# A list schedule that reckons transfers on one shared wire, and eight idle matmuls instead of twelve

## The chip, the cores and the metric

The kernel runs on one core of one Trainium2 chip. The metric is the device time in microseconds; several runs are taken, and their median counts. The core has five instruction streams, each carried out strictly in the order in which the program holds it: TensorE (PE in the profile, with PEld for its weight loads), VectorE (DVE), ScalarE (ACT), GpSimd (POOL) and SyncE (SP). SP and ACT issue the transfers (DMA) from HBM. The streams wait for one another by semaphores.

## What is computed

Two layers of a small transformer on 256 positions of width 1024, in float32. Each layer has a normalisation whose scale, shift and gate come from a conditioning vector `c` (`ada_w`, 1024 × 3072 per layer), a mixer, and a gated residual. The first mixer (nsa) has 16 heads in 4 groups and adds up three attentions: over compressed blocks, over selected blocks and over a window. With 256 positions the selection takes every block. The second (moba) is plain causal attention at this length.

```python
cond = jax.nn.silu(c)
for i in range(DEPTH):                       # DEPTH = 2
    shift, scale, gate = jnp.split(cond @ ada_w[i] + ada_b[i], 3, axis=-1)
    h = rms_norm(x, norm_g[i]) * (1 + scale[:, None, :]) + shift[:, None, :]
    y = nsa_mixer(h, ...) if i % 2 == 0 else moba_mixer(h, ...)
    x = x + gate[:, None, :] * y
# nsa_mixer: q, kc, vc, ks, vs, kw, vw, gl, z = split(h @ w_in)
#   o = g0 * attend(q, compressed) + g1 * attend(q, selected) + g2 * attend(q, window)
# moba_mixer: q, k, v, z = split(h @ w_in);  o = attend(q, k, v)
# both: y = (o * silu(z)) @ w_out
```

## The kernel before

**The work.** Every weight matrix is read from HBM once, in pieces of 256 rows by 512 columns (512 KB) that land in a tile of the ring `raw` (five buffers; `early`, twelve, in the first stage). ACT casts a piece into its high part `hi` (float32r), DVE subtracts to get the low part `lo` (function `parts_of`), and PE multiplies three times: high by high, low part of the weight, low part of the activation `HT`. Rings of four buffers hold `hi` and `lo`. Products add up in PSUM, in the ring `acc` (two buffers: one pair, for the two halves of the positions) or `ps` (six). Function `chunk` takes one slice of 512 output columns through four pieces and then lets ACT copy both accumulators out (for the queries by `raw_part`, into `n_in`); the next chunk needs the two buffers again. The second layer's gate is computed beside the chunks on DVE, from eight more pieces of `ada_w` (`ada_gate`). So the stream of `raw` loads in the second layer alternates between `moba_w_in` and `ada_w`.

**The stages**, as the trace shows them: conditioning, first normalisation and first products (to about 60 us); keys, compression and the rest of the first layer's projections, mixed with the attention of the first layer (to about 190); output projection and second normalisation (to about 230); the second layer's projections (to about 270), attention (to about 310) and output projection.

**What sets the order.** Nothing is issued while the program is described. Class `Plan` records every operation with its engine, a cost in nanoseconds (`_cost`), what it depends on and the tiles that it needs. At the end `Plan.issue` runs a list schedule: each engine has a clock; again and again the operation that can start first by the model is taken (equal starts are decided by a level and then by the order of description), its engine's clock is moved on, and the real instruction is emitted. The engine then holds its instructions in that order for good. The model's times decide nothing but the order and which buffer of a ring a tile gets; at run time an instruction waits for its real semaphores. All instructions are emitted at one line, L354, so the profile names nearly everything L354, and tiles tell operations apart.

In the model an operation's result is seen by others some time after its end (`SEEN`, by engine: T, A, V, G, S are PE, ACT, DVE, POOL, SP). A transfer takes up its issuing engine's clock for its bytes at 360 bytes per nanosecond, at least 450 ns, and its data is seen `SEEN["S"]` later. What waits on SP for another operation gets a hop of 1,220 ns. `START` is each clock's beginning. A ring's buffer is free again when its last reader is done, by the model.

```python
SEEN = {"T": 197.0, "A": 142.0, "V": 128.0, "G": 200.0, "S": 910.0}            # L60
START = {"T": 1500.0, "A": 2000.0, "V": 1500.0, "G": 5800.0, "S": 1750.0}       # L62
return max(450.0, free(aps[0]) * aps[0].shape[0] * 4 / 360.0)                   # _cost of a transfer
seen = end + (self.SEEN["S"] if "dma" in op["calls"][0][0] else self.SEEN[e])   # L332, issue
```

**The idle matmuls.** Twelve multiplications of the 128 × 128 identity by itself into a PSUM tile that nobody reads (`SPINS`, L425) fill PE before there is work. They are recorded at the lowest urgency, so the schedule puts them where PE would else wait. The trace shows each as two matmul records, 24 in all: ten from 1.41 us, six from 4.05 us and eight from 8.46 us.

Of the kernel before, what the change touches and what calls it, by code (L numbers as in the profile page):

```python
# [18 lines left out]
S = 256  # L19
# [15 lines left out]

TICK = 10240 / 3
TILED, LATER = -0.5, 0


class Tag:  # L40
# [9 lines left out]
class Plan:  # L50
# [6 lines left out]

    SEEN = {"T": 197.0, "A": 142.0, "V": 128.0, "G": 200.0, "S": 910.0}  # L60
    AHEAD = 250.0
    START = {"T": 1500.0, "A": 2000.0, "V": 1500.0, "G": 5800.0, "S": 1750.0}  # L62

    def __init__(self, nc):
        self.nc = nc
# [86 lines left out]
    def record(self, engine, method, args, kw):  # L152
        op = self.open or self._new(engine)
        op["engine"] = op["engine"] or engine
        assert op["engine"] == engine
        aps = [a for a in list(args) + list(kw.values()) if isinstance(a, bass.AP)]
        outs = [aps[0]] + ([kw["accum_out"]] if "accum_out" in kw else [])
        for a in aps:
            if not any(a is o for o in outs):
                self._touch(op, a, False)  # L160
        for a in outs:
            self._touch(op, a, True)
        op["calls"].append((method, args, kw))
        op["cost"] += self._cost(engine, method, args, kw, aps)
        if engine == "T":
            op["mode"] = (aps[1].shape[0], aps[1].shape[-1]) if "tile_position" in kw else None
        return op

    def _cost(self, engine, method, args, kw, aps):
        def free(a):  # L170
            n = 1
            for _, k in a.ap[1:]:
                n *= k
            return n

        if "dma" in method:
            return max(450.0, free(aps[0]) * aps[0].shape[0] * 4 / 360.0)
        psum = any(str(a.space).endswith("PSUM") for a in aps)
        n = max(free(a) for a in aps)
        if engine == "T":  # L180
            if method == "transpose":
                return 262.0 if aps[1].dtype == F32 else 180.0
            cols = free(aps[2])
            if aps[2].dtype == F32:
                m = free(aps[1])
                if "tile_position" in kw and m <= 64:
                    return max(cols * 4.28 * max(32, m) / P, 60.0)
                return 2 * max(cols * 2.14, 264.0)
            return max(cols * (1.07 if aps[2].dtype == F32R else 1.0), 264.0)
        if engine == "A":  # L190
            return 0.833 * n + (51.0 if psum else 94.0) + 93.0 * sum(isinstance(kw.get(k), bass.AP) for k in ("bias", "scale", "accum_out"))
        if engine == "G":
            return 1.5 * n + 150.0
        if method == "reciprocal":
            return 6.5 * n + 68.0
        fast = not psum and (method == "tensor_copy" or method.startswith("tensor_scalar"))
        pointers = len(aps) - 2 if method.startswith("tensor_scalar") else 0
        return (0.521 if fast else 1.042) * n + 68.0 + 61.0 * pointers
# [22 lines left out]
    def issue(self, opening=()):  # L221
# [40 lines left out]
                return None  # L262
            return max(min(tag.free)[0], gate["end"] if gate else 0.0)

        clock = dict(self.START)
        tally, mode = {}, None
        ready = {e: [] for e in self.engines}
        for op in ops:
# [4 lines left out]
        while done < len(ops):  # L273
            best = None
            for e, ops_e in ready.items():
                if not ops_e:
                    continue
                found = []
                first = None
                for op in ops_e:  # L280
                    t = max(clock[e], op["at"])
                    if first is not None and t > first and not (op["level"] < 0 and t <= first + self.AHEAD):
                        continue
                    blocked = False
                    for n in op["needs"]:
                        r = room(n)
                        if r is None:
                            blocked = True
                            break
                        t = max(t, r)  # L290
                    if blocked:
                        continue
                    found.append((t, self._rank(op, e, mode), op["id"], op))
                    first = t if first is None else min(first, t)
                pick = min(found, key=lambda f: f[:3]) if found else None
                if pick:
                    soon = [f for f in found if f[1] < 0 and f[1] < pick[1] and f[0] <= pick[0] + self.AHEAD
                            and f[0] < pick[0] + pick[3]["cost"]]
                    if soon:
                        pick = min(soon, key=lambda f: (f[1], f[0], f[2]))  # L300
                if pick and (best is None or pick[0] < best[0]):
                    best = pick + (e,)
            start, _, _, op, e = best
            ready[e].remove(op)
            for n in op["needs"]:
                t = self.tiles[n]
                if t["slot"] is None:
                    tag = t["tag"]
                    gate = closed.get(tag.name)
                    if gate and not gate["called"]:  # L310
                        gate["called"] = True
                        gate["call"]()
                    slot = min(tag.free)
                    tag.free.remove(slot)
                    t["slot"] = slot[1]
                    tag.given.add(t["place"])
                    tag.early.add(t["place"])
                    while tag.next in tag.given:
                        tag.early.discard(tag.next)
                        tag.next += 1  # L320
                    tag.known.clear()
            cost = op["cost"]
            if e == "T":
                tick = int(start // TICK)
                if op["mode"] != mode:
                    cost += 240.0
                mode = op["mode"]
                cost = cost * (1 / 2.4 if tally.get(tick - 1, 0.0) >= 3060.0 else 1 / 1.2)
                tally[tick] = tally.get(tick, 0.0) + op["cost"]
            end = start + cost  # L330
            clock[e] = end
            seen = end + (self.SEEN["S"] if "dma" in op["calls"][0][0] else self.SEEN[e])  # L332
            op["end"], op["begin"] = seen, start
            for n in op["needs"]:
                t = self.tiles[n]
                t["left"] -= 1
                t["end"] = max(t["end"], seen)
                if not t["left"]:
                    t["tag"].free.append((t["end"], t["slot"]))
                    t["tag"].early.discard(t["place"])  # L340
                    t["tag"].done.add(t["place"])
                    t["tag"].known.clear()
                    for g in gates:
                        if t["tag"].name in g["for"]:
                            g["left"] -= 1
                            g["end"] = max(g["end"], t["end"])
            for a in after[op["id"]]:
                b = ops[a]
                b["at"] = max(b["at"], end if e == b["engine"] == "T" else seen + (1220.0 if b["engine"] == "S" else 0.0))
                b["wait"] -= 1  # L350
                if not b["wait"]:
                    ready[b["engine"]].append(b)
            for method, args, kw in op["calls"]:
                r = getattr(self.engines[e], method)(*[self._real(a) for a in args],  # L354
                                                     **{k: self._real(a) for k, a in kw.items()})
            done += 1
# [25 lines left out]
def kernel(  # L382
# [29 lines left out]
    T, A, V, G, Q = plan.T, plan.A, plan.V, plan.G, plan.S  # L412
# [9 lines left out]
        late["pool"] = ctx.enter_context(tc.tile_pool(name="attn", bufs=1))  # L422

    KP = 2
    SPINS = 12  # L425
    START = [("s", 0, 1), ("k", 0), ("s", 1, 1), ("s", 2, 2), ("k", 1), ("s", 4, 2), ("k", 2), ("s", 6, 2), ("k", 3)]
    plan.tag("acc", psum, 512, 2, space="PSUM")
    plan.tag("ps", psum, 512, 6, space="PSUM")
# [474 lines left out]
    FIRST = ((1024, 512), (1536, 512), (2048, 512), (0, 256))  # L903
    load_stage(*START[0])
    load_stage(*START[1], range(2))
    load_stage(*START[2])
    load_stage(*START[1], range(2, 4))
    for _ in small_loads():
# [166 lines left out]
    for kq in range(4):  # L1075
        w1 = [load(bass.AP(tensor=nsa_cmp_w1.tensor, offset=nsa_cmp_w1.offset + kv * 2048 * 256 + kq * 512 * 256,
                           ap=[[256, P], [P * 256, 4], [1, 256]])) for kv in range(2)]
        for k in range(4):
            with plan.at(FILL), plan.group():
                for kv in range(2):  # L1080
                    T.matmul(hid[64 * kv:64 * kv + 64, 0:256],
                             FLAT[kv][kq // 2][:, 4 * (kq % 2) + k].rearrange("p g n -> p (g n)"), w1[kv][:, k, :],
                             start=(kq == 0 and k == 0), stop=(kq == 3 and k == 3), tile_position=(0, 64 * kv))
# [20 lines left out]
    with plan.group():  # L1104
        for cc in range(2):
            T.matmul(cmp_ps[0:64, 0:64], u[:, cc, 0, :], w2[:, 0, cc, :], start=(cc == 0), stop=(cc == 1))
        for m in range(2):
            T.matmul(cmp_ps[0:64, 64:96], selC[:, m].rearrange("p g n -> p (g n)"), TCS[:, m, :],
                     start=(m == 0), stop=(m == 1))
# [22 lines left out]
    for hf in range(2):  # L1132
        for cc in range(2):
# [4 lines left out]
                     start=(cc == 0), stop=(cc == 1))  # L1138
# [237 lines left out]
```

## Time and profile before

| | |
|---|---|
| median of 3 runs | 340.52 us (338.61 to 341.25) |
| the profiled execution's own time | 338.96 us |
| its span, first to last instruction | 337.2 us |
| mean granted TensorE clock | 0.995 |
| busy time of PE, DVE, ACT, POOL | 319.1, 238.8, 195.8, 27.6 us |
| matmul records | 2143 |
| moved by DMA | 66.84 MB, 198 GB/s over the span |

The profile is of one execution. Times are microseconds from the first instruction of the span. In a row of the timeline stand start, duration, engine, line, operation, output and inputs by tile name, shapes and count; in square brackets the engine's idle time just before it and what ended it. In the table of waits stand the engine and tile that waited, what for, and the total, number and longest of the waits. The chain that ended last gives start, duration and what took the time. Matmuls overlap, so a matmul's duration is longer than its distance to the next one: products of 512 columns follow one another every 0.23 us.

### The profile page before, as it was taken

The page shows a single profiled execution, that of the slowest core. Times are in us where ns is not written, and L with a number is a line of the kernel's source. Part 1 is how long each engine was busy: PE and PEld are TensorE (multiplying, and loading weights), DVE is VectorE, ACT ScalarE, POOL GpSimd, SP SyncE. Part 2 cuts the span into 40 slices and gives each one's busy share as a digit, 9 for nine tenths or more (in the row PEclk, how much of TensorE's full clock was granted, in tenths as well). Part 3 has the DMA queues.
Part 4 walks back from the last instruction along what each step waited for, and adds up shares of the span by engine and source line. Part 5 has one row for each costly group of instructions (what it writes and reads, how often), then busy time and mean ns, then how long its engine had stood idle before and what let it go on. Part 6 is the DMA issues. An engine that isn't in the chain of part 4 may idle for free.

```text
span 337.2 us, 5948 instructions
## 1 busy us (share of the span) xinstructions
PE 319.1 (95%) x2143; PEld 252.5 (75%) x2143; DVE 238.8 (71%) x569; ACT 195.8 (58%) x467; POOL 27.6 (8%) x97
## 2 busy tenths in 40 slices
PE   5899999999999889999999999989869999999994
PEld 4675677796577557977979887767657998889883
DVE  1544465789889671986855587897978999974763
ACT  4625235546586555655885673886255799884420
POOL 6000898000000000000000000000000000000000
PEclk9999999999999999999999999999979999999999
DMA  8979998646985492476826338248896330303102
GB/s 252 339 252 367 366 363 276 195 135 211 353 281 213 150 385 77 140 235 225 290 75 240 82 115 278 87 133 280 296 345 200 124 124 1 126 0 137 51 34 93
DMA packets 43876, 66.84 MB, mean 198 GB/s; under 512 B 3799, under 2 KB 20294, under 8 KB 43846
## 3 DMA queue, kind: packets, MB, share of 16 engines
q1 hardware_dynamic: 43678, 66.40, 59.0%
q8 instruction: 17, 0.28, 0.3%
q14 instruction: 13, 0.11, 0.1%
q10 hardware_dynamic: 168, 0.06, 0.1%
HBM read 65.40 MB, written 1.05 MB: 197 GB/s over the span
## 4 chain that ended last, share of the span: by engine, by line
PE 76%; DMA 9%; DVE 8%; ACT 4%; issue 1%; ACTq 1%; SPq 0%; DVEq 0%
PE ps L354 43%; PE acc L354 33%; DMA raw<-in_nsa_w_in_dram 4%; DVE lo L354 2%; DMA y<-in_nsa_cmp_pe_dram 2%; DMA raw<-in_moba_w_in_dram 1%; DMA raw<-in_ada_w_dram 1%; ACT hi L354 1%; ACT p L354 1%; DVE gate L354 1%; DVE tiny L354 1%; DVE rs L354 1%; ACT n_in L354 1%; DVE y L354 1%; ACTq L354 1%
## 5 line engine op out<-in xcount | busy, mean ns | idle before, releaser
L354 ACT CAST hi<-raw 128x1024 fp32r<-128x1024 f32 (+1 forms) x50 | 50.9, 1026 | 35.2 <-PE acc L354 19.2
L354 DVE TENSOR_TENSOR lo<-raw,hi 128x1024 fp32r<-128x1024 f32 (+1 forms) x50 | 59.0, 1185 | 15.7 <-ACT hi L354 15.6
L354 PE MATMUL acc<-hi,HT 128*128 128x512 f32 (+1 forms) x176 | 58.1, 396 | 5.6 <-ACT n_in L354 3.7
L354 PE MATMUL acc<-HT,hi 128*128 128x256 f32 x256 | 51.2, 291 | 0.0
L354 ACT ACTIVATE p<-ps,tiny 128x128 f32<-128x128 f32 (+1 forms) x96 | 39.6, 431 | 11.6 <-DVE tiny L354 11.5
L354 PEld LDWEIGHTS acc<-hi,HT 128*128 128x128 f32 x176 | 33.0, 192 | 15.2 <-ACT n_in L354 4.1
L354 PEld LDWEIGHTS acc<-HT,hi 128*128 128x128 f32 x256 | 40.5, 189 | 1.3 <-DVE g L354 0.8
L354 PE MATMUL acc<-HT,lo 128*128 128x256 f32 x128 | 36.7, 288 | 0.0
L354 PE MATMUL acc<-lo,HT 128*128 128x512 f32 (+1 forms) x88 | 35.5, 404 | 0.3 <-DVE lo L354 0.3
L354 DVE TENSOR_REDUCE tiny<-ps 128x2 f32<-128x512 f32 (+2 forms) x40 | 24.8, 628 | 11.1 <-PE ps L354 10.8
L354 PE MATMUL ps<-KTA,qg 128*128 128x256 f32 (+1 forms) x192 | 30.7, 297 | 0.0
L354 PE MATMUL ps<-hi,HT 128*128 128x512 f32 (+1 forms) x96 | 28.6, 367 | 0.0
L354 PEld LDWEIGHTS ps<-KTA,qg 128*128 128x128 f32 x192 | 26.2, 191 | 2.7 <-issue 1.8
L354 ACT COPY pT<-ps 128x384 f32<-128x384 f32 x48 | 21.1, 497 | 9.2 <-PE ps L354 9.1
L354 PEld LDWEIGHTS acc<-HT,lo 128*128 128x128 f32 x128 | 24.2, 189 | 0.3 <-issue 0.2
L354 PE MATMUL ps<-hi,qg 128*128 128x512 f32 x64 | 22.2, 395 | 0.0
L354 PE MATMUL acc<-hi,qg 128*128 128x512 f32 x64 | 22.0, 394 | 0.0
L354 PE MATMUL ps<-identF,p 128*128 128x128 f32 x144 | 20.7, 276 | 0.3 <-ACT p L354 0.3
L354 ACT ACTIVATION_READ_ACCUMULATOR p<-ps,tiny 128x1 f32 x96 | 20.7, 215 | 0.0
L354 PEld LDWEIGHTS ps<-hi,HT 128*128 128x128 f32 x96 | 17.1, 188 | 4.3 <-issue 1.9
L354 PEld LDWEIGHTS acc<-lo,HT 128*128 128x128 f32 x88 | 17.0, 193 | 3.9 <-DVE lo L354 1.2
L354 PE MATMUL ps<-pT,VA 128*64 128x256 f32 (+1 forms) x192 | 18.9, 334 | 0.0
(194 smaller groups left out, 563.3 us busy)
## 6 DMA issues: line engine op xcount, KB each, us to landing
raw<-in_ada_w_dram SPq DMA_DIRECT2D x32, 512.0 KB, 5.1
raw<-in_moba_w_in_dram SPq DMA_DIRECT2D x20, 512.0 KB, 4.7
early<-in_ada_w_dram SPq DMA_DIRECT2D x16, 512.0 KB, 10.0
early<-in_nsa_w_in_dram SPq DMA_DIRECT2D x12, 512.0 KB, 8.9
raw<-in_nsa_w_in_dram SPq DMA_DIRECT2D x12, 512.0 KB, 5.6
raw<-in_nsa_cmp_w_dram SPq DMA_DIRECT2D x8, 512.0 KB, 4.2
raw<-in_nsa_w_out_dram SPq DMA_DIRECT2D x8, 512.0 KB, 4.9
raw<-in_moba_w_out_dram SPq DMA_DIRECT2D x8, 512.0 KB, 4.2
```

Source lines behind the costliest of these rows:

```text
L354: r = getattr(self.engines[e], method)(*[self._real(a) for a in args], **{k: self._real(a) for k, a in kw.items()})
```

## The change

The model of transfers in `Plan` is replaced. An issue takes 450 ns on ACT whatever its size, and on SP the bytes at 330 bytes per nanosecond, at least 450 ns. A clock `wire`, shared by all transfers, says when the data has passed: not before 450 + 1,500 ns after the start of the issue, and one transfer behind the other at 330 bytes per nanosecond; the data is seen 700 ns after that. The extra hop of 1,220 ns into SP is gone. Results of ACT and DVE are seen 20 ns later than before; ACT and SP begin at 790 ns. `SEEN["S"]` is no longer what a transfer's landing is taken from. And `SPINS` is 8 instead of 12. Apart from the four idle matmuls no operation is added or removed: the same ones are put in an order that the new model gives.

```diff
+ISSUE, FIRST_BYTE, RATE, LANDED = 450.0, 1500.0, 330.0, 700.0
...
-    SEEN = {"T": 197.0, "A": 142.0, "V": 128.0, "G": 200.0, "S": 910.0}
+    SEEN = {"T": 197.0, "A": 162.0, "V": 148.0, "G": 200.0, "S": 200.0}
     AHEAD = 250.0
-    START = {"T": 1500.0, "A": 2000.0, "V": 1500.0, "G": 5800.0, "S": 1750.0}
+    START = {"T": 1500.0, "A": 790.0, "V": 1500.0, "G": 5800.0, "S": 790.0}
...
+        if "dma" in method:
+            op["bytes"] = self.bytes
...
         if "dma" in method:
-            return max(450.0, free(aps[0]) * aps[0].shape[0] * 4 / 360.0)
+            self.bytes = free(aps[0]) * aps[0].shape[0] * 4
+            return ISSUE if engine == "A" else max(ISSUE, self.bytes / RATE)
...
-        clock = dict(self.START)
+        clock, wire = dict(self.START), 0.0
...
-            seen = end + (self.SEEN["S"] if "dma" in op["calls"][0][0] else self.SEEN[e])
+            seen = end + self.SEEN[e]
+            if "bytes" in op:
+                wire = max(wire, start + ISSUE + FIRST_BYTE) + op["bytes"] / RATE
+                seen = wire + LANDED
...
-                b["at"] = max(b["at"], end if e == b["engine"] == "T" else seen + (1220.0 if b["engine"] == "S" else 0.0))
+                b["at"] = max(b["at"], end if e == b["engine"] == "T" else seen)
...
-    SPINS = 12
+    SPINS = 8
```

## The prediction

> **What bounds the kernel now.** First the page's head, for which engine is full.
>
> ```profile
> span 337.2 us, 5948 instructions
> ...
> PE 319.1 (95%) x2143; PEld 252.5 (75%) x2143; DVE 238.8 (71%) x569; ACT 195.8 (58%) x467; POOL 27.6 (8%) x97
> ```
>
> TensorE (PE) is busy for 319.1 of 337.2 us. A new order of the same matmuls can win only what is left, 18.1 us, and what PE loses while busy. Where that lies is read from the table of windows: microseconds, then busy time of each engine, the granted PE clock, the DMA share and GB/s.
>
> ```profile
> core 0: us, PE busy (x) PEld busy (x) DVE busy (x) ACT busy (x) POOL busy (x), PEclk, DMA share, GB/s
> 0.00:20.00 20.00, 14.60 (x119) 12.08 (x120) 8.12 (x31) 11.10 (x19) 5.17 (x32) 1.00 0.89 273
> 20.00:80.00 60.00, 59.97 (x387) 44.72 (x388) 37.00 (x81) 25.35 (x43) 22.47 (x65) 1.00 0.85 275
> 80.00:130.00 50.00, 46.85 (x326) 32.37 (x324) 38.64 (x110) 31.28 (x89) 0.00 (x0) 1.00 0.76 263
> 130.00:210.00 80.00, 80.00 (x607) 66.11 (x604) 54.73 (x127) 50.85 (x139) 0.00 (x0) 1.00 0.54 179
> 210.00:240.00 30.00, 28.70 (x127) 21.42 (x127) 25.70 (x52) 20.91 (x46) 0.00 (x0) 1.00 0.56 181
> 240.00:247.20 7.20, 3.52 (x16) 2.54 (x14) 5.95 (x11) 2.73 (x4) 0.00 (x0) 1.00 0.97 354
> 247.20:252.00 4.80, 4.80 (x15) 3.75 (x16) 4.47 (x9) 2.96 (x4) 0.00 (x0) 0.65 0.90 334
> 252.00:331.00 79.00, 79.00 (x553) 68.50 (x552) 62.47 (x152) 50.56 (x127) 0.00 (x0) 1.00 0.28 92
> 331.00:337.30 6.30, 1.67 (x8) 1.03 (x6) 1.76 (x3) 0.00 (x0) 0.00 (x0) 1.00 0.22 83
> ```
>
> PE is idle for 5.4 us at the start, 3.2 us from 80 to 130, 1.3 us from 210 to 240, 3.7 us from 240 to 247, and 4.6 us at the end, where the last output is written. From 247.2 to 252 it has 0.65 of its clock, which costs 0.35 × 4.8 = 1.7 us more. Everywhere else it never stops. PE's waits from 80 to 130, and from 236 to 262 (total, times, longest):
>
> ```profile
> PE ps L354 <- ACT p L354: 1.2, 2, 0.9
> PE acc L354 <- DMA raw<-in_nsa_cmp_w_dram: 0.6, 1, 0.6
> PE ps L354 <- DVE pc L354: 0.6, 1, 0.6
> PE acc L354 <- ACT hi L354: 0.5, 1, 0.5
> PE acc L354 <- DVE lo L354: 0.3, 1, 0.3
> ```
>
> ```profile
> PE acc L354 <- ACT n_in L354: 3.7, 1, 3.7
> ```
>
> The last one is the largest. PE at both ends of it, ACT in the meantime, and from the chain and the table of transfers the two loads ahead:
>
> ```profile
> 243.03 0.39 PE L354 MATMUL acc<-hi,HT 128*128 128x512 f32 x1
> 247.10 0.50 PE L354 MATMUL acc<-hi,HT 128*128 128x512 f32 x1 [3.68 <-ACT n_in L354]
> ```
>
> ```profile
> 241.87 1.05 ACT L354 CAST hi<-raw 128x1024 fp32r<-128x1024 f32 x1 [3.30 <-DMA raw<-in_moba_w_in_dram]
> 245.52 1.04 ACT L354 CAST hi<-raw 128x1024 fp32r<-128x1024 f32 x1 [2.60 <-DVE gate L354]
> 246.47 1.07 ACT L354 COPY n_in<-acc 128x512 f32<-128x512 f32 x2
> ```
>
> ```profile
> 237.24 4.53 DMA raw<-in_moba_w_in_dram
> ```
>
> ```profile
> raw<-in_moba_w_in_dram SPq DMA_DIRECT2D x1, 512.0 KB, 5.2
> ```
>
> PE finished the `acc` pair at 243.42 and needed a free one. ACT had been free since 242.92, but the next instruction in its fixed order was a cast of a weight tile. That tile's load was issued at 240.24 (the last row is that one load, 5.2 us to landing), so it landed at 245.4. The cast is put down to a gate instruction that ended then too. Both evictions of `acc` stood behind it. This is an error of the planner's order, and its size can be read: before, the schedule takes such a load for 524,288 / 360 + 910 = 2,366 ns. The rows show 4.5 and 5.2 us. The same between 108 and 122 us:
>
> ```profile
> 108.54 4.93 DMA raw<-in_nsa_w_in_dram
> ...
> 115.88 3.73 DMA raw<-in_nsa_w_in_dram
> ```
>
> ```profile
> 113.55 1.05 ACT L354 CAST hi<-raw 128x1024 fp32r<-128x1024 f32 x1 [2.01 <-DMA raw<-in_nsa_w_in_dram]
> ...
> 119.64 1.05 ACT L354 CAST hi<-raw 128x1024 fp32r<-128x1024 f32 x1 [1.32 <-DMA raw<-in_nsa_w_in_dram]
> ```
>
> ACT stands 2.0 and 1.3 us in front of casts whose loads took 4.9 and 3.7 us, with softmax exponentials queued behind them; PE's waits for `p` and `pc` (1.2 + 0.6 us) follow.
>
> **The change part by part.**
>
> *Later landings.* A 512 KB load is now reckoned 450 + 1,500 + 524,288 / 330 + 700 = 4,239 ns from issue to landing, 1,873 ns more. Against the four rows above (3.7 to 5.2 us) the old figure is 1.4 to 2.8 us early, the new one 0.5 us late to 1.0 us early. No instruction is added or removed. Loads of `raw` are all issued from SP in program order within one ring of five buffers, so SP's order can hardly change; what changes is where casts (ACT), low parts (DVE) and products (PE) stand among other work.
>
> (1) The wait at 243. If the second cast comes behind the evictions, these run once PE is done: the first `acc` (its last matmul is six before the end, 6 × 0.23 = 1.4 us earlier) after the cast that ends at 242.92, free near 243.5. The pause falls from 3.7 to about 0.3 us, and the 1.7 us of slow clock behind it goes. What is late next: PE then has two pieces at hand, cast at 237.5 and 241.87, of 12 matmuls each, 2 × 12 × 0.23 = 5.5 us, to 249.1; the third is cast at 245.52 and is ready. From 252 to 331 PE never stops, so an earlier start should carry to the end. Bounds: 0 (the order stays) to −5.4. I take −5.0, nearest the row, since old landings undershoot by 2.8 us here.
>
> (2) Waits from 80 to 130: 1.8 us behind the casts, 0.8 us for `hi` and `lo`, 0.6 us for a load itself. Bounds 0 to −3.2. A new belief of 4.2 us does not cover a load of 4.9, and the 0.6 us is a transfer that stays late: I take −1.5, near half.
>
> (3) *Hops 20 ns longer* (ACT, DVE), the hop of 1,220 ns into SP dropped, ACT and SP begun at 790 ns. The two queues' first transfers do start at 0.79 in the trace. The dropped hop touches the four output writes, which nothing follows on SP. These only break ties: 0, with (5).
>
> (4) *Eight idle matmuls for twelve.* Each is two records.
>
> ```profile
> 8.46 1.96 PE L354 MATMUL ps<-identF 128*128 128x128 f32 x8
> 10.36 1.94 PE L354 MATMUL ps<-early,condz 128*32 128x128 f32 x32
> 12.22 1.50 PE L354 MATMUL ps<-identF,n_in 128*128 128x128 f32 x8
> 13.56 0.28 PE L354 MATMUL ps<-selP,row 128*128 128x2 f32 x2
> 13.70 1.07 PE L354 MATMUL ps<-identF,n_in 128*128 128x128 f32 x8
> ```
>
> ```profile
> 11.04 0.75 DVE L354 TENSOR_SCALAR n_in<-X,rs 128x1024 f32<-128x1024 f32 x1
> ```
>
> The last four, 1.96 us, run just ahead of the modulation matmuls. Without them those could start near 8.7, but the transposes of `n_in` wait for DVE until 11.79, so at most 12.22 − 11.79 = 0.4 us reaches the path. Against it: eight transposes take 1.50 us and the next eight 1.07 us, so PE gets faster near 13, and less work before may put that off. The nearest price is the 1.7 us that the slow stretch at 247 cost. Bounds −0.4 to +1.7; I take 0, as PE mostly waits for others there.
>
> The Trainium skill, "TensorE: Matmul & The Clock Gate", Part 1 (the warmup section), speaks against this part: the clock stays halved until about 3.4 us of sustained activity, in a free-running window. The speed-up near 13 us and the 0.65 clock after 3.7 us of idling agree with it; by that rule a missed window would make the sum 1.7 us longer.
>
> (5) *New waits.* Every engine's order is rebuilt, and a new order has mistakes of its own. Of today's PE idle between 20 and 331 us (0.03 + 3.15 + 1.30 + 3.68 = 8.2 us), 3.7 + 1.8 + 0.8 = 6.3 us come from early casts, and 1.9 us from other causes. Bounds 0 to +5.4 (one more wait like that at 243); I take +1.5, near those 1.9.
>
> Sum: −5.0 − 1.5 + 0 + 0 + 1.5 = −5.0 us. The profiled execution took 338.96 us (its span and 1.76 us around it), so 334.0; the runs' median, 340.52, is 1.56 us above it, so the forecast for the median is 335.5. The three runs lie within 338.6 to 341.25, so under 1% (3.4 us) can hardly be told from no change.
>
> **The rivals.**
>
> - *Casts and evictions move together* (the change does not do what it says). Around 240 us the transfers run at a 0.97 share, so every landing may move in the plan and PE's end of the chunk with it; the cast stays in front. For it: both depend on the same stream of loads. Against: PE had two cast pieces in hand, so its end does not hang on the newest load. Waits stay; part (2) alone and new waits cancel: 340.0.
> - *A colder start*: part (4) at its worst, +1.7: 335.5 + 1.7 = 337.2. For: the speeds at 12 and 13.7 us. Against: nothing on PE is urgent until 16 us.
> - *Casts too late, loads starved*: slower. A raw buffer is given back after cast and low part; if these now stand behind chain work, the next load is issued later.
>
> ```profile
> raw<-in_moba_w_in_dram SPq DMA_DIRECT2D x13, 512.0 KB, 4.9
> raw<-in_ada_w_dram SPq DMA_DIRECT2D x7, 512.0 KB, 4.4
> ```
>
> Between 221 and 260 us 20 loads go out through five buffers, four rounds. If each round slips by the 1.87 us of added belief, 7.5 us come on top, in place of the 3.7 us wait: 340.5 + 7.5 − 3.7 = 344.3. It decides from where the slip per round passes the wait that it replaces, 3.7 / 4 = 0.9 us. For: the share of 0.97 leaves no slack. Against: loads really take 4.4 to 5.2 us, longer than the new belief, so casts are still placed rather early than late.
> - *All order waits go and nothing new comes*: 3.7 + 1.7 + 1.8 + 0.8 = 8.0 us less, 332.5.
>
> **How the numbers follow.** Chances: forecast 0.46 (its own range 332 to 338.5), together 0.25, starved 0.14, colder start 0.10, all gone 0.05. The likeliest is the forecast, 335.5. A range of 331 to 343 leaves out the starved case's larger half and a little below 331. Faster by over 1% (below 337.1): 0.44 of the forecast's 0.46, all of "all gone", half of the colder start, hardly any of "together": 0.55. Within 1%: the rest of these two and most of "together": 0.30. Slower (above 343.9): most of "starved" and the worst of "together": 0.15.
>
> **What would show it.** Right: near 243 us an eviction of `acc` on ACT ahead of the cast that waits longest, no PE wait of over 1 us from 236 to 260, granted clock 1.00 there, ACT's waits for loads from 104 to 126 shorter than 3.3 us in all, PE busy still near 317 to 318 (four idle matmuls less). Wrong: a wait of the old size at a new place, PE idle between loads from 225 to 260 with a DMA share under 0.8, or the second eight transposes still at 1.5 us.

## The result, and the profile after

The changed kernel takes 330.75 us (median of 4, 329.93 to 331.21), the kernel before 340.29 (median of 4 beside it): ratio 0.972, 95% interval 0.968 to 0.977. The forecast was 335.5, with a range of 331 to 343: the result lies 0.25 us below the range; the direction and the wait at 243 us came as forecast, the size did not. Times and ratios from here on leave out one execution each of the kernel before (342.95 us), spins_only (342.12) and landed_m1173 (349.07), which fell into a slower state of the chip. Between the two profiled executions, 338.96 and 330.94 us, lie 8.0 us. The head of the page after:

```profile
span 329.2 us, 5934 instructions
## 1 busy us (share of the span) xinstructions
PE 314.0 (95%) x2135; PEld 249.9 (76%) x2135; DVE 239.5 (73%) x569; ACT 196.0 (60%) x467; POOL 25.7 (8%) x97
```

PE's idle time fell only from 18.1 to 15.2 us; its busy time fell by 5.1, though only the eight records of four idle matmuls, 1.96 us in the trace before, are gone. To find the place, the start of the same matmul is taken in both traces. Five of them cut the program into six stages:

| stage, from … to the start of … | before, us | after, us | difference |
|---|---|---|---|
| first instruction … first `acc<-raw,p` (hidden layer of the compression) | 77.10 | 77.22 | +0.12 |
| F: … 17th `acc<-hi,qg` (first layer's attention, into its output projection) | 128.03 | 124.26 | −3.77 |
| … 109th `acc<-hi,HT` of 512 columns | 36.73 | 36.62 | −0.11 |
| Q: … last `acc<-hi,HT` of 512 columns (second layer's keys and queries) | 20.45 | 15.28 | −5.17 |
| … last `acc<-HT,hi` (gates `z`, second attention) | 48.04 | 48.93 | +0.89 |
| … last product | 21.93 | 21.94 | +0.01 |

Stage Q holds the wait at 243 us of the prediction. The table of windows for just this stage, before and then after (columns as above):

```profile
241.86:262.31 20.45, 16.77 (x66) 12.57 (x65) 17.23 (x36) 10.91 (x14) 0.00 (x0) 0.92 0.81 274
```

```profile
238.10:253.40 15.30, 15.25 (x67) 11.47 (x66) 14.25 (x30) 10.92 (x14) 0.00 (x0) 1.00 0.85 288
```

The same work (one matmul record more or less at the edges) takes 5.15 us less: idle time is down from 3.68 to 0.05 us, and the granted clock is up from 0.92 to 1.00, which is 0.08 × 20.45 = 1.6 us. ACT's timeline there shows the new order:

```profile
238.13 1.05 ACT L361 CAST hi<-raw 128x1024 fp32r<-128x1024 f32 x1 [2.85 <-DVE rs L361]
239.09 1.20 ACT L361 COPY n_in<-acc 128x512 f32<-128x512 f32 x2
240.32 1.06 ACT L361 ACTIVATE n_out<-n_in 128x1024 f32<-128x1024 f32 x1
241.28 1.03 ACT L361 CAST hi<-raw 128x1024 fp32r<-128x1024 f32 x1
243.51 1.05 ACT L361 CAST hi<-raw 128x1024 fp32r<-128x1024 f32 x1 [1.20 <-DMA raw<-in_moba_w_in_dram]
```

One cast, not two, stands ahead of the two evictions (`n_in<-acc`); the next stand behind them, and PE has no wait at all from 236 to 262 us. Stage F, before and after:

```profile
77.10:205.13 128.03, 124.88 (x935) 96.60 (x935) 92.00 (x238) 82.18 (x230) 0.00 (x0) 1.00 0.60 204
```

```profile
77.22:201.47 124.25, 122.25 (x935) 95.73 (x935) 94.02 (x240) 83.45 (x231) 0.00 (x0) 1.00 0.63 215
```

Of 3.8 us, 1.15 are idle time (3.15 to 2.00). The other 2.6 are busy time of the very same 935 matmuls, at a granted clock of 1.00 both times. A matmul's record is longer than the distance to its successor, so a pause shorter than the overlap leaves no idle time. For one group, from 77 to 90 us before and 77 to 91 after:

```profile
L354 PE MATMUL acc<-raw,p 128*64 128x256 f32 x64 | 8.3, 385 | 0.6 <-DMA raw<-in_nsa_cmp_w_dram 0.6
```

```profile
L361 PE MATMUL acc<-raw,p 128*64 128x256 f32 x64 | 7.6, 384 | 0.0
```

64 equal matmuls with equal mean durations: 0.6 us of waits that show, and 0.7 us within what counts as busy. Of these 0.4 can be seen to be a pause, in the trace before:

```profile
77.80 2.98 PE L354 MATMUL acc<-raw,p 128*64 128x256 f32 x26
...
81.72 0.65 PE L354 MATMUL acc<-raw,p 128*64 128x256 f32 x2
82.99 1.94 PE L354 MATMUL acc<-raw,p 128*64 128x256 f32 x14 [0.62 <-DMA raw<-in_nsa_cmp_w_dram]
```

The 26 of the first row take 0.23 us for every two; the two ahead of the wait count as busy for 0.65. The other 2.2 us of busy time in F are not traced to a cause: they may be such pauses too, or lie in which matmuls stand next to one another.

### The profile page after: what moved, and what is told of

It reads as the page before. It is cut to its first block, busy times and chain, and to the rows that moved or that the text cites. A ratio compares the mean times of both kernels' runs of the same rounds, so it can differ in the third digit from the quotient of the medians.

```text
span 329.2 us, 5934 instructions
## 1 busy us (share of the span) xinstructions
PE 314.0 (95%) x2135; PEld 249.9 (76%) x2135; DVE 239.5 (73%) x569; ACT 196.0 (60%) x467; POOL 25.7 (8%) x97
## 4 chain that ended last, share of the span: by engine, by line
PE 80%; DVE 8%; DMA 6%; ACT 3%; issue 1%; ACTq 0%; SPq 0%
PE ps L361 44%; PE acc L361 36%; DMA early<-in_nsa_w_in_dram 3%; DMA raw<-in_nsa_w_out_dram 2%; DMA y<-in_nsa_cmp_b_dram 2%; DVE rs L361 1%; ACT hi L361 1%; DVE n_out L361 1%; DVE lo L361 1%; DVE y L361 1%; DVE tiny L361 1%; ACT p L361 1%; DVE X L361 1%; DVE KTA L361 1%; ACTq L361 0%
## 5 line engine op out<-in xcount | busy, mean ns | idle before, releaser
L361 PE MATMUL acc<-HT,hi 128*128 128x256 f32 x256 | 49.0, 286 | 1.0 <-DVE zT L361 1.0
L361 PEld LDWEIGHTS acc<-hi,HT 128*128 128x128 f32 x176 | 32.2, 188 | 8.5 <-issue 1.1
L361 PE MATMUL acc<-lo,HT 128*128 128x512 f32 (+1 forms) x88 | 34.0, 387 | 0.0
```

## The experiments

**Theories.** "Late landings": the gain is the planner's belief about when loads land, through the place of casts among other work. Rivals: the gain is in the rest of the change (hops, starts, idle matmuls, wire); any changed number redraws every engine's order, and after is a lucky draw; the gain at one place is given back behind it. All ratios are to the kernel before, beside which each ran; F and Q are the stages above, of each run's profiled execution.

| kernel | 512 KB load reckoned to land after, ns | median us | ratio (95%) | F | Q |
|---|---|---|---|---|---|
| before | 2,366 | 340.29 | 1 | 128.0 | 20.4 |
| spins_only | 2,366 | 339.56 | 0.996 (0.992 to 1.000) | 128.4 | 20.0 |
| before_hops | 2,366 | 339.29 | 0.999 (0.996 to 1.001) | 127.8 | 21.9 |
| all_but_landing | 2,366 | 343.51 | 1.008 (1.004 to 1.012) | 132.6 | 20.2 |
| landed_m1173 | 2,366 | 344.86 | 1.014 (1.008 to 1.020) | 134.6 | 19.3 |
| after | 4,239 | 330.75 | 0.972 (0.968 to 0.977) | 124.3 | 15.3 |
| land_only | 4,239 | 331.74 | 0.975 (0.972 to 0.978) | 125.0 | 15.7 |
| land_hops | 4,239 | 332.67 | 0.979 (0.975 to 0.983) | 125.7 | 15.5 |
| hops_mid | 4,239 | 332.88 | 0.979 (0.976 to 0.981) | 127.1 | 15.0 |
| hops_more | 4,239 | 333.28 | 0.980 (0.973 to 0.987) | 127.2 | 15.2 |
| no_wire | 4,239 | 330.10 | 0.972 (0.966 to 0.978) | 124.2 | 15.1 |
| after_spins12 | 4,239 | 333.71 | 0.981 (0.975 to 0.987) | 124.3 | 15.0 |
| rate_360 | 4,106 | 333.92 | 0.982 (0.976 to 0.987) | 126.0 | 15.8 |
| landed_1700 | 5,239 | 334.70 | 0.984 (0.981 to 0.987) | 126.4 | 15.0 |
| landed_2700 | 6,239 | 333.80 | 0.982 (0.979 to 0.985) | 127.8 | 15.1 |
| late_first | 4,239, first half | 335.25 | 0.986 (0.982 to 0.990) | 124.0 | 20.3 |
| late_second | 4,239, second half | 336.57 | 0.990 (0.987 to 0.993) | 128.6 | 15.6 |
| evict_first | 2,366 | 339.14 | 0.998 (0.996 to 1.001) | 129.0 | 17.4 |

**land_only and all_but_landing: the change in two.**

```diff
-    SEEN = {... "S": 910.0}
+    SEEN = {... "S": 2783.0}        # land_only: this alone
```

```diff
-    SEEN = {"T": 197.0, "A": 142.0, "V": 128.0, ...}; SPINS = 12
+    SEEN = {"T": 197.0, "A": 162.0, "V": 148.0, ...}; SPINS = 8      # all_but_landing
-    START = {... "A": 2000.0, ... "S": 1750.0}
+    START = {... "A": 790.0, ... "S": 790.0}
-    seen + (1220.0 if b["engine"] == "S" else 0.0)
+    seen
```

> The kernel before, with one number changed: the data of a transfer is reckoned 2,783 ns after its issue instead of 910, so that a 512 KB load lands 4,239 ns after issue as in the changed kernel; twelve idle matmuls, old hops, old starts. Theory 'late landings': nearly the whole gain, 7 to 9.5 us less than before. Theory 'hops and starts': within 3 us of before. Theory 'any new order is a new draw': anywhere from 328 to 342.

> The kernel before with all the rest of the change: eight idle matmuls, hops of ACT and DVE 20 ns longer, starts at 790 ns, no extra hop into SP; transfers are reckoned as before. Theory 'late landings': within 2.5 us of before, waits of ACT in front of casts as before. Theory 'hops and starts': 6 to 9 us less. Theory 'new draw': anywhere from 328 to 342.

One number brings 331.74, nearly the whole gain. All the rest without it brings 343.51, slower than before, and 1 us beyond what the theory gave it; ACT waits 13.0 us there for loads of `nsa_w_in`, not 7.0 as in the kernel before. The gain is the landing's.

**spins_only: eight idle matmuls alone.**

```diff
-    SPINS = 12
+    SPINS = 8
```

> The kernel before with eight idle matmuls instead of twelve and nothing else. Theory 'late landings': within 2 us of before; the start alone costs 0 to 1.7 us by a later full clock. Theory 'new draw': up to 5 us either way, since the planner's clock for PE starts differently and the order of every engine shifts.

339.56, an interval that touches 1: no difference that these runs can tell. The redraw moved nothing by more than 0.5 us in F and Q.

**landed_m1173, landed_1700, landed_2700: the landing earlier and later, in the changed kernel.**

```diff
-ISSUE, FIRST_BYTE, RATE, LANDED = 450.0, 1500.0, 330.0, 700.0
+ISSUE, FIRST_BYTE, RATE, LANDED = 450.0, 1500.0, 330.0, -1173.0     # 1700.0; 2700.0
```

> The changed kernel with LANDED = -1,173 instead of 700: everything new (wire, rate, hops, starts, eight idle matmuls), but a 512 KB load is reckoned to land 2,366 ns after issue, as before. Theory 'late landings': the gain is gone, 337 to 343. Theory 'wire and the rest': within 2 us of the changed kernel's 330.75. Theory 'any new order is a new draw': anywhere from 328 to 343.

> The changed kernel with LANDED = 1,700: a 512 KB load lands 5,239 ns after issue, as the slower loads of the trace do. Theory 'late landings': no worse than the changed kernel, 328 to 332, with ACT's waits in front of casts shorter still. Theory 'casts too late starve the loads' : 333 or more. Theory 'new draw': 328 to 343.

> The changed kernel with LANDED = 2,700: landing 6,239 ns after issue, 1 to 2.5 us later than most loads of the trace. Theory 'late landings': the optimum is passed, 330 to 335. Theory 'casts too late starve the loads': 335 or more, with PE idle between 200 and 260 us and a lower share of the transfers there. Theory 'new draw': 328 to 343.

With the old landing everything else of the change makes the kernel slower than before (344.86, 1.9 us above the range expected). One and two microseconds later than the changed kernel cost 4.0 and 3.1 us; landed_1700 misses the 328 to 332 expected of the theory. In its trace 2.8 of these 4.0 us are lost before stage F (80.02 against 77.22 us), with a granted clock of 0.58 from 10 to 20 us and 0.83 from 30 to 40, and 2.2 in F; in that of landed_2700 3.6 are lost in F. A redraw of the order by ten nanoseconds of hop moves F by 2.9 us, and the kernel with twelve idle matmuls loses the same 2.9 us ahead of F (both below), so a cost of the later belief itself is not shown. What follows the belief is ACT's time in front of casts. In the tables of waits of landed_m1173, before, after and landed_2700, for the loads of `nsa_w_in` (total, times, longest):

```profile
ACT hi L361 <- DMA raw<-in_nsa_w_in_dram: 11.2, 5, 5.8
```

```profile
ACT hi L354 <- DMA raw<-in_nsa_w_in_dram: 7.0, 6, 2.0
```

```profile
ACT hi L361 <- DMA raw<-in_nsa_w_in_dram: 2.3, 2, 1.3
```

```profile
ACT hi L361 <- DMA raw<-in_nsa_w_in_dram: 1.4, 1, 1.4
```

landed_1700 stands out of this row with 4.3 us, but ACT's waits for loads into `raw` from all matrices fall throughout: 20.8, 12.9, 9.0, 6.5 (landed_1700) and 1.4 us. The wait goes on falling where the time no longer does: past 4.2 us, less waiting on ACT no longer shortens the kernel. The starved loads of the rival are not seen: Q stays at 15.0 us up to a belief of 6.2 us.

**hops_mid, hops_more, before_hops, land_hops: how much is chance.**

```diff
-    SEEN = {"T": 197.0, "A": 162.0, "V": 148.0, ...}
+    SEEN = {"T": 197.0, "A": 152.0, "V": 138.0, ...}     # hops_mid; 172, 158: hops_more
-    SEEN = {"T": 197.0, "A": 142.0, "V": 128.0, ...}
+    SEEN = {"T": 197.0, "A": 152.0, "V": 138.0, ...}     # before_hops; with "S": 2783.0: land_hops
```

> The changed kernel with ACT's and DVE's hops 10 ns shorter (152 and 138 ns), a change of the model far below any wait that the trace shows. Theory 'late landings': within 2 us of the changed kernel's 330.75. Theory 'new draw': up to 6 us off, most likely upward. The distance tells how much of a difference between two orders is chance.

> The changed kernel with ACT's and DVE's hops 10 ns longer (172 and 158 ns), one more draw of the order with the same landings. Theory 'late landings, plus chance of the order': 329 to 334, the second layer's stage again 15 to 15.7 us, the first layer's attention stage anywhere between 124 and 128 us. Theory 'the hops are tuned': 334 or more.

> The kernel before with ACT's and DVE's hops 10 ns longer (152 and 138 ns), landings as before: another draw of the order at the early landing. Theory 'landings': the first layer's attention stage 128 to 135 us, the second layer's stage 19 to 20.5, 338 to 346 in all. Theory 'chance of the order': as likely 333 as 343.

> The kernel before with the later landing (2,783 ns) and the hops of before_hops: the same redraw at the late landing. Theory 'landings': 124 to 128 us and 15 to 16 us in the two stages, 330 to 335 in all, at least 6 us under before_hops. Theory 'chance of the order': no such distance.

Ten nanoseconds of hop move the changed kernel by 2.1 and 2.5 us, nearly all in F (127.1 and 127.2 instead of 124.3): that is the size of chance between two orders. Even one order does not repeat exactly: the kernel before, late_second and evict_first (below) issue the same instructions in the same order on every engine up to 204 us, and F took 128.0, 128.6 and 129.0 us, so a difference of 1 us in F is not read. The pair with one redraw and two landings differs by 6.6 us, as theory said. hops_more lies within its range, hops_mid 0.1 us outside. before_hops is as slow as expected, with F (127.8) 0.2 us below and Q (21.9) 1.4 us above what was expected. So after is one of the better draws at its landing, but each of the ten kernels with 4.1 us or more in the whole program is below each of the five at the old landing (330.1 to 334.7 against 339.3 to 344.9 us).

**no_wire, rate_360: the parts of the new transfer model.**

```diff
-                wire = max(wire, start + ISSUE + FIRST_BYTE) + op["bytes"] / RATE
-                seen = wire + LANDED
+                seen = start + ISSUE + FIRST_BYTE + op["bytes"] / RATE + LANDED     # no_wire
-ISSUE, FIRST_BYTE, RATE, LANDED = 450.0, 1500.0, 330.0, 700.0
+ISSUE, FIRST_BYTE, RATE, LANDED = 450.0, 1500.0, 360.0, 700.0                      # rate_360
```

> The changed kernel without the shared wire: each transfer is reckoned to land 450 + 1,500 + bytes/330 + 700 ns after its own issue, whatever else is under way. SP's clock already spaces its 512 KB loads 1,589 ns apart, so only the first loads, issued beside ACT's, are reckoned differently. Theory 'late landings': 330 to 333.5, the stage from the end of the first key chunk to the second layer's last key and query product unchanged. Theory 'the shared wire is the gain': 336 or more.

> The changed kernel with transfers reckoned at 360 bytes per ns instead of 330 (a 512 KB load lands 4,106 ns after issue). Theory 'late landings': 329.5 to 333.5, the second layer's stage as short as in the changed kernel (15 to 15.7 us from product 108 to the last). Theory 'the slower rate is the gain': 336 or more.

Without the shared wire it is 330.10, no different from after. It could hardly be: the order is the same on ACT, DVE, POOL and SP from start to end, and on PE it differs only between 24 and 32 us. So the wire adds next to nothing here, and no_wire is no second draw. With the old rate it is 333.92, 0.4 us outside what was expected but still 0.982, with Q at 15.8, 0.1 above the range: within the size of chance.

**after_spins12: twelve idle matmuls in the changed kernel.**

```diff
-    SPINS = 8
+    SPINS = 12
```

> The changed kernel with twelve idle matmuls. Theory 'idle matmuls do nothing': 329.5 to 333.5, the first product of the first layer within 1 us. Theory 'fewer idle matmuls leave PE cold at the start': 329 to 330, the full clock granted a window (3.4 us) earlier than with eight.

333.71, 3.0 us more than after, 0.2 above the first range, and the place speaks against both theories: F and Q are equal, and the difference lies before the first `acc<-raw,p` (80.09 against 77.22 us). Windows of twelve, and then of eight:

```profile
10.00:20.00 10.00, 8.88 (x81) 6.82 (x73) 5.25 (x16) 6.72 (x11) 0.00 (x0) 0.66 0.94 285
20.00:30.00 10.00, 10.00 (x70) 7.11 (x68) 2.63 (x6) 0.97 (x3) 0.00 (x0) 1.00 1.01 345
30.00:40.00 10.00, 9.12 (x39) 5.62 (x39) 6.63 (x14) 4.35 (x6) 5.59 (x12) 0.83 1.08 364
```

```profile
10.00:20.00 10.00, 8.70 (x89) 6.95 (x90) 6.35 (x17) 7.28 (x12) 0.00 (x0) 1.00 0.92 273
20.00:30.00 10.00, 10.00 (x70) 6.82 (x69) 1.89 (x10) 1.83 (x4) 0.00 (x0) 1.00 1.02 349
30.00:40.00 10.00, 10.00 (x57) 6.38 (x59) 6.35 (x12) 3.03 (x4) 6.90 (x18) 1.00 1.08 360
```

With twelve, PE's clock is withdrawn in two stretches, at a mean of 0.66 from 10 to 20 us and 0.83 from 30 to 40. More idle matmuls did not keep it. The 1.00 of the kernel with eight at the start is not full speed, though; the same 30 matmuls run there at 10 and at 16 us:

```profile
10.05 1.93 PE L361 MATMUL ps<-early,condz 128*32 128x128 f32 x30 [0.99 <-DMA early<-in_ada_w_dram]
...
16.37 1.07 PE L361 MATMUL ps<-early,condz 128*32 128x128 f32 x30 [0.63 <-DMA early<-in_ada_w_dram]
```

So near 10 us PE is slow with eight as well (with twelve the 30 matmuls at 9.53 us took 1.07), and the column of the clock says little ahead of about 15 us. The stretch from 30 to 40 us is the plainer loss: 0.17 × 10 = 1.7 us. Over the four executions of twelve the mean granted clock was 0.985, 0.978, 0.978 and 0.993, and the last of these was the shortest (332.02); with eight it was 0.986 to 1.000, and the times there (329.93 to 331.21) do not follow it. Whether the order that goes with twelve causes this, or these executions met it by chance, is not shown.

**late_first, late_second: the later landing in one half.**

```diff
+    plan.second = len(plan.ops)        # ahead of the first output projection
-            seen = end + (self.SEEN["S"] if "dma" in ... else self.SEEN[e])
+            seen = end + ((2783.0 if op["id"] < self.second else self.SEEN["S"]) if "dma" in ... else self.SEEN[e])
                                        # late_first; late_second: >=
```

> The kernel before, with a transfer's data reckoned 2,783 ns after its issue instead of 910 for all that is described ahead of the first output projection, 910 behind it. Theory 'landings in both halves': the first layer's attention stage 124 to 127.5 us (before: 128.0), the second layer's stage 19 to 20.5 us as before, 335 to 338 in all. Theory 'the first layer's share is chance': that stage 128 or more, 339 to 342.

> The kernel before, with the later landing only for what is described from the first output projection on; the order of the first layer stays as before up to there. Theory 'landings in both halves': the second layer's stage 15 to 16 us instead of 20.4, of which 0.5 to 1.4 us are lost behind it, 335 to 337 in all. Rival 'the gain there is given back later', as with the one order edge: 338 or more.

Stage F and Q of late_first, and then of late_second:

```profile
77.58:201.59 124.01, 122.09 (x935) 95.64 (x935) 95.08 (x240) 83.53 (x231) 0.00 (x0) 1.00 0.63 218
```

```profile
238.21:258.49 20.28, 16.73 (x66) 12.57 (x65) 17.09 (x37) 11.02 (x14) 0.00 (x0) 0.92 0.85 284
```

```profile
79.60:208.24 128.64, 125.27 (x936) 96.79 (x936) 92.03 (x239) 82.97 (x231) 0.00 (x0) 1.00 0.59 202
```

```profile
244.88:260.44 15.56, 15.26 (x67) 11.40 (x65) 14.79 (x31) 10.70 (x14) 0.00 (x0) 1.00 0.86 300
```

Each half gets its own stage and leaves the other as before. The halves gain 4.9 and 3.6 us against the 340.18 us beside them, 8.5 together; land_only, both halves, gained 8.2. So F's share comes with the landings too, and Q's reaches the end.

**evict_first: one order edge.**

```diff
             A.copy(hi, t)["deps"].update(behind)          # parts_of, in the kernel before
...
-    chunk(m_in, ((512, 512),), raw_part(raw_q, 512), spread=1)
+    chunk(m_in, ((512, 512),), raw_part(raw_q, 512), spread=1, behind=evicted[-2:])   # its third piece only
```

> The kernel before, with one order edge added in the planner: the cast of the third weight piece of the second query chunk (second layer) must come behind the evictions of the first query chunk's accumulators. Theory 'late landings' (the wait near 243 us and the slow clock behind it are one ordering error of ACT): 4.5 to 5.5 us less than before, no PE wait over 1 us from 236 to 260, granted clock 1.00 there. Rival 'transfers bind there' (share 0.97): PE waits for the next load instead, under 1.5 us gained.

Neither theory's number: 339.14, 0.998 (0.996 to 1.001). The evictions do come first, and the wait of 3.7 us is gone:

```profile
243.55 1.05 ACT L354 CAST hi<-raw 128x1024 fp32r<-128x1024 f32 x1 [2.95 <-DMA raw<-in_moba_w_in_dram]
244.50 1.25 ACT L354 COPY n_in<-acc 128x512 f32<-128x512 f32 x2
```

```profile
PE acc L354 <- DVE lo L354: 1.5, 1, 1.5
PE ps L354 <- ACT y L354: 0.2, 1, 0.2
```

Q falls by 3.0, not 5: the low part of the next piece is late in DVE's order, and PE waits 1.5 us for it. Behind Q the rebuilt order of the gates and the second attention takes 49.4 instead of 48.0 us. So one corrected edge leaves the planner's belief wrong for the casts and low parts around it; of the 3.0 us 1.6 are left behind Q, and 0.8 between the medians. The two profiled executions took the same time (338.96 and 339.03 us), because the one of evict_first reached the end of F 1.8 us later in the same order, with a granted clock of 0.82 and 0.76 in the two stretches from 30 to 38 us. That the new order behind Q is what takes the 1.4 us is read from the stages only; a kernel that keeps that order was not tried.

## Why the prediction was wrong, point by point

*Term (1), the wait at 243 us, −5.0:* right. Stage Q gave 5.2, idle 3.6 and clock 1.6, and in all eleven kernels with the later landing there it lies from 15.0 to 15.8 us, against 19.3 to 21.9 at the old one (17.4 with the single edge).

*Term (2), the waits from 80 to 130 us, −1.5 with bounds of 0 to −3.2:* this is the step that failed. Stage F gave 3.8, more than its bound. The bound was made of the idle time that the table of windows shows; that part came out near the forecast (idle time in F fell by 1.15 us). The prediction also named "what PE loses while busy", gave it no term outside the slow stretch at 247 us, and said that PE "never stops" elsewhere. The other 2.6 us of F lay there, and PE was busy for 314.0 us after the change, not the 317 to 318 that the prediction named as a sign of being right. Of the 2.6 us 0.4 are shown to be a pause; the cause of the rest stays open. The other draws put F's gain between 0.2 and 4.0 us, so part of the miss is the draw, and that after is one of the better ones is luck; none of the eleven with the later landing there was slower than before in F.

*Term (3), 0 for hops, starts and the dropped hop:* right only in company. With the later landing they add nothing measurable (330.75 against 331.74); without it they belong to a kernel 3.5 us slower than before.

*Term (4), 0 for the idle matmuls, bounds −0.4 to +1.7:* right on the kernel before (0.996, 0.992 to 1.000). In the changed kernel eight instead of twelve are worth 3.0 us, outside the bound, all of it ahead of 80 us. The start of the profile shows both sides of the term: two modulation matmuls 1.9 us earlier (the other thirty 0.3), but the second eight transposes at 1.45 us instead of 1.07, which the prediction had named as a sign of being wrong, and the first product 1.2 us later. At 77 us the two traces differ by 0.1.

*Term (5), +1.5 for new waits:* 0.9 behind Q, of which 1.0 is one wait of PE for `zT`; and stage F has a new one of its own:

```profile
PE ps L361 <- ACT y L361: 1.2, 1, 1.2
PE ps L361 <- ACT p L361: 0.4, 1, 0.4
PE ps L361 <- DVE n_parts L361: 0.3, 1, 0.3
```

*The step from the profile to the median:* the sum gave 334.0 for the profiled execution, and 1.56 us were added because the median before lay that far above its profile. After, the median lies 0.2 us below it. Of the 4.75 us between forecast and result, 3.0 are terms, 1.75 this step. The two profiled executions lie 8.0 us apart where the medians lie 9.5: the distance of one execution from a median is scatter of the kernel before, and adding it to the forecast carried it over.

*The rivals:* the starved case and "together" did not come; "all gone" came nearest (332.5). Even that was 1.75 us too high; it counted the idle time that shows and the slow stretch at 247 us, not the rest of PE's busy time.

## What to carry to other kernels

Where a planner fixes each engine's order, its belief about when a load lands can be worth more than the order at one place: here one number gave 8.2 us, one corrected edge hardly 1. A belief 1.4 to 2.8 us too early put instructions that wait for loads ahead of instructions that could run; one that was 1 to 2 us later than the changed kernel's took 3 to 4 us more, hardly beyond chance, and still less than the time before. And a change of order is worth judging by several draws, with numbers of the model moved by nothing that matters: at the landing of the changed kernel they lay up to 3.6 us apart (330.10 to 333.71). Busy time of PE is no floor for such a change: that of the same 935 matmuls fell by 2.6 us.

## What the runs showed of the hardware

PE's clock is withdrawn at different moments in executions of one order. The trace of late_second runs the same order as the kernel before up to the first output projection, yet comes to the first `acc<-raw,p` 2.5 us later. About 1.0 us of this is there by 29 us, where the same 16 matmuls (`ps<-early,condz`) start at 28.93 instead of 27.89. The rest comes with the next slow stretch: one `acc<-lo,HT` starts at 37.62 instead of 35.12. From 34 to 38 us the row of late_second is

```profile
34.00:38.00 4.00, 4.00 (x12) 2.83 (x11) 3.17 (x6) 0.53 (x2) 3.29 (x5) 0.59 1.09 348
```

a granted clock of 0.59 without idle time on PE, which is 0.41 × 4.0 = 1.6 us, and in the trace before

```profile
34.00:38.00 4.00, 4.00 (x29) 2.63 (x30) 2.86 (x5) 0.00 (x0) 3.91 (x8) 1.00 1.08 364
```

The Trainium skill, "TensorE: Matmul & The Clock Gate", Part 1, says that the window of the gate runs free, so that a kernel meets it at another phase each time; the scatter agrees. It has the clock fall after an idle window; the row of late_second shows fewer than half the matmuls but no idle time.

The clock explains only part of the scatter. Over 48 executions of the kernel before (337.4 to 342.34 us), the five with a mean granted clock of 0.998 to 0.999 took 337.8 us in the median and the six with 0.979 to 0.985 took 341.3, but the 37 between show no such order: 339.8 at 0.988 to 0.990, 340.1 at 0.992 to 0.995. The one profiled before (338.96 us, 0.995) was among the shorter ones; that its 1.56 us below the median are of this kind is not shown.
